# Hymba block in float32 on one core: weight quarters split in step with the products, a last block in two groups of 256 positions, differences on VectorE

## The chip, the cores and the metric

The kernel runs on one core of a Trainium2 chip. The metric is the device time of one execution in microseconds (us). The engines are TensorE (PE, with its weight loads shown apart as PEld), VectorE (DVE), ScalarE (ACT), GpSimd (POOL) and SyncE (SP), which here issues nearly all DMAs. Each engine takes its instructions in the order in which they were put, and waits at one whose data or buffer isn't ready.

## The reference, cut to what matters

```python
def reference(x, norm1_g, w_in, w_gate_up, b_gate, gla_norm_g, conv_w, w_out,
              norm2_g, w_ffn_gate, w_ffn_up, w_ffn_down, norm_f_g):   # x: (1, 2048, 1024) float32
    h = rmsnorm(x, norm1_g)
    p_q, p_k, p_v, p_g, p_a, c_b, c_c, c_h = split(h @ w_in)
    log_a = log_sigmoid(p_a @ w_gate_up + b_gate) / 16
    o = rmsnorm(gla_chunked(p_q * 64 ** -0.5, p_k, p_v, log_a), gla_norm_g) * silu(p_g)
    o_conv = c_b * causal_depthwise_conv(c_c * c_h, conv_w)
    x = x + concat([o, o_conv]) @ w_out
    h2 = rmsnorm(x, norm2_g)
    x = x + (silu(h2 @ w_ffn_gate) * (h2 @ w_ffn_up)) @ w_ffn_down      # hidden width 2816
    return rmsnorm(x, norm_f_g)
```

## The kernel before

Features lie on the 128 partitions and positions along the free axis, in blocks of 512. Two blocks are a half. The stages are the input projection with the two mixers (gated linear attention and the short convolution), the output projection, the FFN's up stage, its down stage and the last norm, and the first four of them run half by half.

**Products.** Float32 operands are split into a high and a low part of the type fp32r, and one product of 128 by 128 weights is three matmuls over 512 columns: high by high, high by low, low by high (L460, L461 and L462 in `product_step`). The big products are made in units. A unit has 2 by 2 blocks of weights and 2 by 2 blocks of operands (two feature blocks by two position blocks) and follows Strassen and Winograd with seven products in place of eight, in the order A11·B11, S1·T1, S2·T2, A12·B21, S3·T3, S4·B22, A22·T4. Each has four steps of three matmuls in the projections and the up stage, and two or three steps in the down stage. A PSUM bank takes each product's sum; ACT copies the first ones out (`copied`, L500), and DVE adds the others to these copies (`plus`, L489). In the down stage all of them are added on DVE.

**Weights.** One DMA of 768 KB or 1 MB (L148, `raw_weights`) brings the four quarters of a unit. `unit_weights` makes the sums of quarters that Strassen and Winograd need on DVE (`mix`, L435) and splits each of the seven results with `weight_quarter`: ACT rounds it to the high part (L193), DVE subtracts to the low one (L194). The pool `wq` holds four such split quarters and the pool `raw` two units' raw weights. A unit's seven splits stand in the program ahead of its products; how far each engine takes them up early is left to the scheduler, which orders each engine's instructions by a simulated timeline. `behind(...)` and `issue_after` add an order of issue, without a wait, on top of it.

**Operands.** The operand sums T1 to T4 are made by `combine` (differences: `subtract`, L359). Those of the second half's projection, and of the second half's FFN (`load_h2`), are stored to DRAM and loaded again, partly to be split again on arrival (L193 with `op<-op`).

**The last block.** The FFN's last unit (`last_unit`) isn't made with seven products: it makes feature blocks 6 and 7 of position blocks 2 and 3 of the four blocks (j = 0 and 1 in the code) as plain products, four columns of 36 matmuls over 512 positions in all: two for j = 0, two for j = 1. Then come, for each j, the add to the residual (L1508), the square (L1511), sums of squares over all features by matmuls of one column (L1454), the factor 1/sqrt by Ln, Exp and a Newton step (`factors`, L1463 to L207), its spreading over the partitions (L1467, transposes L1474, a copy for POOL L1475), eight scalings (L1480) on DVE and POOL and eight stores on SP.

## Time and profile before

| | us |
|---|---|
| median of 3 runs | 2055.72 (2054.32 to 2055.76) |
| the profiled execution, its own time | 2050.15 |
| its span in the trace | 2048.4 |
| PE busy | 2021.6 (99%) |
| DVE busy | 1549.0 (76%) |
| ACT busy | 971.7 (47%) |
| POOL busy | 335.4 (16%) |
| DMA | 422.54 MB, mean 206 GB/s |

A group of instructions is shown as line, engine, operation, output<-input by the program's names, shapes, count | busy us, mean ns of one | idle time of the engine ahead of them, and what ended most of it. A row of waits reads: engine, what waited <- what it waited for: us in all, times, the longest. In a timeline the bracket at a row's end is the idle time ahead of the instruction and what ended it. A matmul's shown length is that of its whole passage, and successive ones overlap; the distance between their starts is what each costs.

### The profile page before, as it was taken

Reading aid. Unit: us, or ns where it says so; the run is one execution under the profiler, and the core shown is the slowest. Engines: PE = TensorE matmul, PEld = TensorE weight load, DVE = VectorE, ACT = ScalarE, POOL = GpSimd, SP = SyncE. Lnnn points to the kernel's source line nnn. Section 1 sums busy time; section 2 is a strip of 40 time slices with the busy share of each in tenths; the row PEclk is TensorE's granted clock in tenths of the full one; section 3 lists DMA queues with packets and bytes.
Section 4 is the critical chain, followed back from the end, with each engine's and each line's share of the span. In section 5 each row is a group of like instructions: output and inputs, shape, how many; then the busy total and the mean of one; then the engine's idle time right before and its main releaser. Section 6 shows DMA issues by size and latency. Waiting matters only on the chain.

```text
span 2048.4 us, 26987 instructions
## 1 busy us (share of the span) xinstructions
PE 2021.6 (99%) x9271; PEld 1662.2 (81%) x9271; DVE 1549.0 (76%) x2533; ACT 971.7 (47%) x1930; POOL 335.4 (16%) x218
## 2 busy tenths in 40 slices
PE   9999999999999999999999999999999999999997
PEld 8788878887888888888788888877888888888886
DVE  7888967558744797778777688877777768778884
ACT  6664556755533344444444452334534443453344
POOL 0000000000002451222222112200311321211213
PEclk9999999999999999999999999999999999999998
DMA  7356886425586873546445576576444434586663
GB/s 262 123 201 215 295 301 188 132 85 160 180 307 233 324 270 134 194 150 216 176 145 193 212 285 250 188 277 273 155 169 170 167 136 170 185 328 221 236 231 114
DMA packets 189738, 422.54 MB, mean 206 GB/s; under 512 B 19904, under 2 KB 65184, under 8 KB 180128
## 3 DMA queue, kind: packets, MB, share of 16 engines
q1 hardware_dynamic: 189600, 420.81, 58.5%
q8 instruction: 73, 1.20, 0.2%
q14 instruction: 65, 0.53, 0.1%
HBM read 276.02 MB, written 144.70 MB: 205 GB/s over the span
## 4 chain that ended last, share of the span: by engine, by line
PE 87%; DVE 4%; DMA 4%; ACT 2%; issue 1%; SPq 1%; POOL 0%; DVEq 0%; ACTq 0%; POOLq 0%
PE mm L460 25%; PE mm L462 25%; PE mm L461 25%; PE mm L1220 2%; PE mm L1221 2%; PE mm L1223 2%; DMA raw<-in_wffn_dram 1%; DVE wq L194 1%; DVE h L894 1%; PE a_ps L976 1%; PE mm L756 1%; PE mm L758 1%; PE mm L757 1%; DMA raw<-in_win_dram 1%; PE o_ps L1144 1%
## 5 line engine op out<-in xcount | busy, mean ns | idle before, releaser
L460 PE MATMUL mm<-op,wq 128*128 128x512 f32 x2467 | 961.5, 392 | 10.9 <-ACT c L500 5.0
L461 PE MATMUL mm<-op,wq 128*128 128x512 f32 x2467 | 959.7, 390 | 0.2 <-DVE op L194 0.2
L462 PE MATMUL mm<-op,wq 128*128 128x512 f32 x2467 | 948.7, 390 | 0.9 <-DVE wq L194 0.6
L193 ACT ACTIVATE wq<-raw 128x512 fp32r<-128x512 f32 (+2 forms) x612 | 355.7, 587 | 582.5 <-PE mm L462 461.3
L194 DVE TENSOR_TENSOR wq<-raw,wq 128x512 fp32r<-128x512 f32 (+2 forms) x612 | 446.8, 736 | 165.1 <-ACT wq L193 163.5
L460 PEld LDWEIGHTS mm<-op,wq 128*128 128x128 f32 x2467 | 463.5, 188 | 115.3 <-ACT c L500 6.8
L462 PEld LDWEIGHTS mm<-op,wq 128*128 128x128 f32 x2467 | 463.5, 188 | 99.6 <-DVE wq L194 2.7
L461 PEld LDWEIGHTS mm<-op,wq 128*128 128x128 f32 x2467 | 463.6, 188 | 96.4 <-DVE op L194 1.7
L1202 POOL TENSOR_TENSOR ssx<-ssx,q 128x512 f32<-128x512 f32 x52 | 75.7, 1473 | 866.4 <-ACT q L1201 866.2
L489 DVE TENSOR_TENSOR c<-mm,c 128x512 f32<-128x512 f32 x196 | 134.6, 687 | 52.3 <-PE mm L462 44.9
L489 DVE TENSOR_TENSOR y<-mm,y 128x512 f32<-128x512 f32 x185 | 126.3, 686 | 47.8 <-PE mm L462 47.5
L435 DVE TENSOR_TENSOR raw<-raw 128x512 f32<-128x512 f32 (+2 forms) x192 | 151.9, 794 | 2.9
L1336 POOL TENSOR_TENSOR t<-c,c 128x512 f32<-128x512 f32 x44 | 74.4, 1690 | 434.8 <-DVE c L1332 406.9
L500 ACT ACTIVATE c<-mm 128x512 f32<-128x512 f32 x198 | 115.6, 587 | 17.5 <-PE mm L462 13.9
L435 DVE TENSOR_TENSOR s<-raw 128x512 f32<-128x512 f32 (+2 forms) x96 | 62.0, 645 | 52.0 <-DMA raw<-in_wffn_dram 36.5
L1220 PE MATMUL mm<-op,wq 128*128 128x512 f32 x256 | 101.2, 396 | 0.0
L1221 PE MATMUL mm<-op,wq 128*128 128x512 f32 x256 | 99.7, 390 | 0.0
L193 ACT ACTIVATE wq<-s 128x512 fp32r<-128x512 f32 (+2 forms) x96 | 56.3, 586 | 90.9 <-PE mm L462 88.2
L1418 POOL TENSOR_TENSOR y<-x,y 128x512 f32<-128x512 f32 x32 | 57.7, 1803 | 230.4 <-DVE y L489 181.3
L1223 PE MATMUL mm<-op,wq 128*128 128x512 f32 x256 | 80.0, 390 | 0.0
L435 DVE TENSOR_TENSOR raw<-s,raw 128x512 f32<-128x512 f32 (+2 forms) x96 | 69.8, 727 | 2.0
L552 ACT ACTIVATE c<-c 128x512 f32<-128x512 f32 x78 | 49.2, 631 | 34.7 <-DVE c L489 32.7
(229 smaller groups left out, 1788.5 us busy)
## 6 DMA issues: line engine op xcount, KB each, us to landing
raw<-in_wffn_dram SPq DMA_DIRECT2D x44, 1024.0 KB, 6.1
sa_B<-so SPq DMA_DIRECT2D x47, 512.0 KB, 4.3
op<-sa_B SPq DMA_DIRECT2D x47, 512.0 KB, 6.9
raw<-in_win_dram SPq DMA_DIRECT2D x22, 1024.0 KB, 5.5
sa_T<-so SPq DMA_DIRECT2D x44, 512.0 KB, 3.8
op<-sa_T SPq DMA_DIRECT2D x44, 512.0 KB, 6.4
raw<-in_wdown_dram SPq DMA_DIRECT2D x24, 768.0 KB, 5.8
sx<-y SPq DMA_DIRECT2D x48, 256.0 KB, 4.4
```

The costliest lines, as they stand in the source:

```text
L193: last_hi[:] = [act.activation(hi, src, AF.Copy)]
L194: last_lo[:] = [dve.tensor_tensor(lo, src, hi.bitcast(F32), ALU.subtract)]
L435: dve.tensor_tensor(*args)
L460: pe.matmul(o[:], wh, xh, start=first and k == 0, stop=False, skip_group_check=True)
L461: pe.matmul(o[:], wh, xl, start=False, stop=False, skip_group_check=True)
L462: return pe.matmul(o[:], wl, xh, start=False, stop=k == n - 1, skip_group_check=True)
L489: last_plus[:] = [dve.tensor_tensor(t[:], o[:], t[:], ALU.add)]
L500: last_out[:] = [act.activation(t[:], o[:], AF.Copy)]
L1202: pool.tensor_tensor(ssq[:], ssq[:], q[:], ALU.add)
L1220: pe.matmul(o[e, j][:], wh, m[:, 0, :], start=k == 0, stop=False)
L1221: pe.matmul(o[e, j][:], wh, m[:, 1, :], start=False, stop=False)
L1223: pe.matmul(o[e, j][:], wl, ops[k][j][:, 0, :], start=False, stop=k == KD - 1)
```

## The change

There are three parts.

1. `subtract` in `combine` puts all differences on DVE. Before, they went to POOL outside a stage in which `with_marks` is set.

2. For most units (nine of the first half's projection, all twelve of the second half's, and all units of the FFN in both halves) the weights no longer come from `unit_weights` but from a generator `weight_flow` that runs through all of them in one line. It makes one quarter's job at a time, and a job needs a credit: there are four at the start, and each product gives one back when its copy or add has been issued (`freed`; for units of 256 columns two quarters share a buffer, and every second product gives one). Each job is issued behind the last copy and the last add (`behind(last_out + last_plus)`), and a quarter's sums go into the same job: the first sum behind A11's split, the next two ahead of S1's split. The raw weights of the next unit are loaded where the jobs of the present unit begin. `load_h2` and `ffn_down` tie their loads to other raw loads accordingly.

3. `last_unit` divides the second of its position blocks into two groups of 256 (p0, p1; the first block is j0). Their columns are made by 72 matmuls over 256 positions in place of 36 over 512. Each engine's order is written out by hand (`then`), all of p1 is scaled on DVE, and its stores alternate between the queues of SP and ACT, as are those of p0 that POOL scales put on ACT's queue.

```diff
         def subtract(y, a, b):
             with behind(last_plus if with_marks else []):
-                (dve if with_marks else pool).tensor_tensor(y, a, b, ALU.subtract)
+                dve.tensor_tensor(y, a, b, ALU.subtract)
...
+    def weight_flow():
+        following = Begun(plan.popleft())
+        while following is not None:
+            u, following = following, None
+            begun_units.append(u)
+            if plan:
+                following = Begun(plan.popleft())
+            raw, w, n = u.raw, u.w, u.raw.shape[-1]
+            a11, a12, a22, a21 = [raw[:, i, :] for i in range(4)]
...
+                jobs = [
+                    ("A11", a11, [(s1, a21, a22, ALU.add)]),
+                    ("S1", s1, [(a21, a11, a21, ALU.subtract), (a11, s1, a11, ALU.subtract)]),
+                    ("S2", a11, ()), ("A12", a12, ()),
+                    ("S3", a21, [(a12, a12, a11, ALU.subtract)]), ("S4", a12, ()),
+                    ("A22", a22, ()),
+                ]
+            for i, (name, part, sums) in enumerate(jobs):
+                yield not (u.narrow and i % 2)
+                with behind(last_out + last_plus):
+                    if name == "S1":
+                        for job in sums:
+                            dve.tensor_tensor(*job)
+                    w[name] = weight_quarter(part)
+                    if name != "S1":
+                        for job in sums:
+                            dve.tensor_tensor(*job)
...
+        def freed(i):
+            if flows and flowing:
+                if not current.narrow or i % 2 or i == len(PRODUCTS) - 1:
+                    credits[0] += 1
+                advance()
...
         oa = mul(0)
         c11 = copied("c11", oa, (0, 0))
+        freed(0)
...
-    def last_unit(src, ops, b12, y, ssq):
-        raw = raw_weights(src)
-        w = [weight_quarter(raw[:, i, :]) for i in (0, 1, 3, 2)]
+    def last_unit(ops, b12, y, ssq):
+        w = [begun_units[0].w[i] for i in (0, 1, 3, 2)]
+        HB = PB // 2
+        parts = {"j0": (0, 0, PB), "p0": (1, 0, HB), "p1": (1, HB, HB)}
...
+        taken("p1", 0, columns_of("p1", 0))
+        add_up("p0", ssq[1])
+        factors("p0", lambda: scale("j0", 1, dve, sp))
+        gained_in("p1", 0)
+        summed("p1", 0, dve)
+        o = columns_of("p1", 1)
+        spread("p0", copied=False)
+        add_up("p1", ssq[1], last=False)
+        taken("p1", 1, o)
+        add_up("p1", q[1, 1], first=False)
+        for d in (3, 7):
+            scale("j0", d, dve, sp)
+        factors("p1", *[partial(scale, "p0", d, dve, sp) for d in (0, 1)])
+        copy_of("p0")
+        gained_in("p1", 1)
+        for d in (2, 5, 6, 7):
+            scale("p0", d, pool, ac)
+        scale("p0", 3, dve, sp)
+        spread("p1", copied=False)
+        scale("p0", 4, dve, sp)
         for d in range(KD):
-            scale(1, d, None if d in (2, 5) else rb1)
+            scale("p1", d, dve, ac if d % 2 else sp)
```

Since a scheduler sets the order, three places show what moves. The first is on ACT in the second half's projection. `ee` are decay factors loaded from DRAM, which ACT turns into exponentials for the attention; `c12` is the third copy of a unit, and `wq` are weight splits. Before:

```order
L1105 ACTIVATE ee_4889<-ee_4889 128x256 [waits DMAHW5_49]
L1106 ACTIVATE ee_4889<-ee_4889 128x256 [waits Activation_49]
L193 ACTIVATE wq_4806<-raw_4784 128x512 [waits DVE_49]
L193 ACTIVATE wq_4809<-raw_4784 128x512 [waits PE_49]
L193 ACTIVATE wq_4998<-raw_4995 128x512 [waits DMAHW7_49,PE_49]
L1023 ACTIVATE el_4741<-g2_4745 128x4 [waits DVE_49]
L1105 ACTIVATE ee_5037<-ee_5037 128x256 [waits DMAHW5_49,DMAHW4_49]
L1106 ACTIVATE ee_5037<-ee_5037 128x256 [waits Activation_49]
L500 ACTIVATE c12_4872<-mm_4812 128x512 [waits DVE_49]
```

Here the copy stands last, behind both pairs of exponentials and four other rows. With the change:

```order
L193 ACTIVATE wq_4856<-raw_4473 128x512 [waits DVE_49]
L1104 ACTIVATE el_4758<-g2_4762 128x4 [waits DVE_49]
L574 ACTIVATE c12_4871<-mm_4804 128x512 [waits DVE_49,PE_49]
L193 ACTIVATE wq_4873<-raw_4473 128x512
L193 ACTIVATE wq_4916<-raw_4671 128x512 [waits DMAHW7_49,PE_49]
L1187 ACTIVATE ee_4894<-ee_4894 128x256 [waits DMAHW5_49,DMAHW1_49]
L1188 ACTIVATE ee_4894<-ee_4894 128x256 [waits Activation_49]
L193 ACTIVATE wq_4935<-s1_4878 128x512 [waits DVE_49,PE_49]
L1187 ACTIVATE ee_5029<-ee_5029 128x256 [waits DMAHW6_49,DMAHW5_49]
L1188 ACTIVATE ee_5029<-ee_5029 128x256 [waits Activation_49]
```

The copy of `c12` stood behind the exponentials of two `ee` tiles, and now stands ahead of both. (The line numbers differ between the two kernels: L500 became L574, L1105 and L1106 became L1187 and L1188.)

The second place is on DVE where the first half's down stage ends and the second half's up stage begins. `y` are the adds of the down stage's products, `s1` and `raw` the sums of quarters, and the wait on DMAHW2_49 is that of the raw weights of the first up unit. Before:

```order
L489 TENSOR_TENSOR y_11037<-mm_12455,y_11037 128x512 [waits PE_49]
L194 TENSOR_TENSOR wq_12544<-raw_12532,wq_12544 128x384 [waits Activation_49]
L435 TENSOR_TENSOR s1_12719<-raw_12717 128x512 [waits DMAHW2_49,DVE_49]
L435 TENSOR_TENSOR raw_12717<-raw_12717 128x512 [waits DVE_49]
L489 TENSOR_TENSOR y_11115<-mm_12560,y_11115 128x512 [waits PE_49]
L194 TENSOR_TENSOR wq_12547<-raw_12532,wq_12547 128x384 [waits Activation_49]
L435 TENSOR_TENSOR raw_12532<-raw_12532 128x384 [waits DVE_49]
```

Here both sums of the new unit stand ahead of an add and of the low part `wq_12547`. With the change (L489 became L557, L435 became L494):

```order
L494 TENSOR_TENSOR raw_12384<-raw_12384 128x384 [waits DVE_49]
L557 TENSOR_TENSOR y_11147<-mm_12567,y_11147 128x512 [waits PE_49,Pool_49]
L194 TENSOR_TENSOR wq_12578<-raw_12384,wq_12578 128x384 [waits Activation_49]
L557 TENSOR_TENSOR y_11145<-mm_12552,y_11145 128x512 [waits PE_49]
L194 TENSOR_TENSOR wq_12591<-raw_12384,wq_12591 128x384 [waits Activation_49]
L557 TENSOR_TENSOR y_11145<-mm_12597,y_11145 128x512 [waits PE_49]
L494 TENSOR_TENSOR s1_12596<-raw_12489 128x512 [waits DMAHW2_49]
L194 TENSOR_TENSOR wq_12608<-raw_12489,wq_12608 128x512 [waits Activation_49]
```

The sum `s1` of the new stage's first unit now stands behind the last low part (`wq_12591`) and three adds of the old stage's last unit.

The third place is SP's queue where the second half's projection begins: loads of stored operands (`op<-si...`), the stores of the mixer's results (`sm`), small attention loads (`gt`), and a unit's raw weights. Before:

```order
L148 DMA op_2864<-siB21_3_456 128x1024 [waits DMAHW5_49,PE_49]
L148 DMA op_2866<-siT3_0_457 128x512 [waits DMAHW6_49,PE_49]
L148 DMA op_2868<-siT3_1_458 128x512 [waits DMAHW7_49,PE_49]
L151 DMA sm0_2_203<-hi_2811 128x512 [waits DMAHW0_49,Activation_49]
L148 DMA op_2870<-siT3_2_459 128x512 [waits DMAHW1_49,PE_49]
L148 DMA op_2872<-siT3_3_460 128x512 [waits DMAHW2_49,PE_49]
L151 DMA sm0_2_203<-c11_2398 128x512 [waits DMAHW3_49,DVE_49]
L148 DMA op_2874<-siB22_0_461 128x512 [waits DMAHW4_49,PE_49]
L148 DMA op_2876<-siB22_1_462 128x512 [waits DMAHW5_49,PE_49]
L148 DMA op_2878<-siB22_2_463 128x512 [waits DMAHW6_49,PE_49]
L148 DMA op_2880<-siB22_3_464 128x512 [waits DMAHW7_49,PE_49]
L148 DMA raw_3044<-in_win_dram 128x2048 [waits DMAHW0_49]
```

Here the raw weights come last. With the change, first the rows from the raw weights on:

```order
L148 DMA raw_2760<-in_win_dram 128x2048 [waits DMAHW5_49,DVE_49]
L148 DMA gt_3081<-sg0_0_153 128x128 [waits DMAHW6_49]
L148 DMA op_2886<-siT3_0_457 128x512 [waits DMAHW7_49,PE_49]
L148 DMA op_2888<-siT3_1_458 128x512 [waits DMAHW0_49,PE_49]
L148 DMA op_2890<-siT3_2_459 128x512 [waits DMAHW1_49,PE_49]
```

The loads of T3 now follow the raw weights. Two rows further on, on the same queue, come the loads of B22 up to the store of `c11`:

```order
L148 DMA op_2894<-siB22_0_461 128x512 [waits DMAHW4_49,PE_49]
L151 DMA sm0_2_203<-hi_2831 128x512 [waits DMAHW5_49,Activation_49]
L148 DMA op_2896<-siB22_1_462 128x512 [waits DMAHW6_49,PE_49]
L148 DMA op_2898<-siB22_2_463 128x512 [waits DMAHW7_49,PE_49]
L148 DMA op_2900<-siB22_3_464 128x512 [waits DMAHW0_49,PE_49]
L151 DMA sm0_2_203<-c11_2390 128x512 [waits DMAHW1_49,DVE_49]
```

The raw weights' load (1 MB) went from behind the loads of B22 to ahead of those of T3, and the store `sm0_2<-c11` from ahead of the four loads of B22 to behind them. Two loads of `gt` were moved up between them.

250 lines of the change are left out of this document (173 added, 77 removed).

## The prediction

> **What bounds the kernel now.** I read the busy times first, then TensorE's waits, then the chain of waits at the end, and last the timeline around each longer wait.
>
> ```profile
> span 2048.4 us, 26987 instructions
> PE 2021.6 (99%) x9271; PEld 1662.2 (81%) x9271; DVE 1549.0 (76%) x2533; ACT 971.7 (47%) x1930; POOL 335.4 (16%) x218
> ```
>
> TensorE is the bound, so the change can win only where TensorE stands still, or where nothing is left for it, at the end. Its waits by cause:
>
> ```profile
> PE mm L460 <- ACT c L500: 5.0, 3, 3.0
> PE mm L460 <- ACT op L193: 2.1, 1, 2.1
> ...
> PE mm L460 <- DVE c L489: 1.5, 3, 0.7
> PE mm L460 <- ACT wq L193: 1.2, 3, 0.5
> ...
> PE mm L460 <- DVE y L489: 0.8, 1, 0.8
> PE mm L462 <- DVE wq L194: 0.6, 1, 0.6
> ```
>
> These add up to 11.2 us. Only 1.8 us of it (the rows of wq) is TensorE waiting for split weights, so a better pace of splitting has little to win directly. What it can do is move other work on ACT and DVE. The splits themselves run early: in the waits of all engines ACT's splits wait for TensorE to free a buffer, 367 times, 1.5 us each.
>
> ```profile
> ACT wq L193 <- PE mm L462: 549.5, 367, 4.1
> DVE s L435 <- DMA raw<-in_wffn_dram: 36.5, 19, 4.1
> ```
>
> The profiled execution took 2050.15 us for a span of 2048.4, and the median shown is 2055.72. I make the sum on the span and add 2055.72 - 2048.4 = 7.3 us for the median.
>
> **Term 1, the end.** The chain of waits from the last product's add on, and the stores:
>
> ```profile
> 2033.75 0.70 DVE y L1508
> 2034.47 0.64 ACT q L1511
> ...
> 2036.86 0.18 DVE rs L205
> ...
> 2037.46 0.44 DVE rep L1467
> ...
> 2037.94 1.13 PE rb_ps L1474 x4
> ...
> 2041.07 2.39 DVE y L1480 x4
> ```
> ```profile
> L151 SPq DMA_DIRECT2D out_dram<-y x16: 332/405/590, 2032.1 to 2044.4; - x16
> DMA to landing us min/median/max: 2.1/2.5/3.4
> ```
>
> From the add at 2033.75 to the last scaling's end at 2043.46 are 9.7 us, and the stores take the 4.9 us to the end: a queue that issues one store in 0.41 us, then a landing of about 2.5. Half-width operations and pitches come from these rows (the first from the down stage's quarters, the second from TensorE's weight loads in the last 40 us):
>
> ```profile
> L435 DVE TENSOR_TENSOR s<-raw 128x256 f32<-128x256 f32 x8 | 3.3, 417 | 1.5 <-DMA raw<-in_wdown_first_dram 1.5
> L462 PEld LDWEIGHTS mm<-op,wq 128*128 128x128 f32 x33 | 6.2, 188 | 1.3
> ```
>
> The four scalings follow each other at 2.39 / 4 = 0.60 us, so one of 256 should follow at 0.33 (0.417 less the same overlap of 0.09). The new order after the last columns of p1: add 0.42; DVE then scales two whole blocks of j0, 1.28, in which the square and the two last column sums hide; mean and eps 0.17; two scalings of p0 while ACT makes Ln and Exp, 0.75; Newton step 0.60 (three rows like the 0.18 one, with gaps); spreading over 256 positions 0.30; two more scalings of p0, 0.78, beside two transposes (1.13 / 2 = 0.56); eight scalings of p1, 2.75. Sum 7.05, against 9.7: a gain of 2.66. Of the 4.9 us to the end, two queues can save at most the backlog of issues, 2044.4 - 2043.46 and one issue, some 1.3 us. Gain between 2.66 and 4.0, taken 3.3.
>
> Against it stand 72 matmuls over 256 positions for 36 over 512. No row has such a matmul. The 512 ones follow at 0.2265 us (472.56, 472.79 below; 0.227 all over the busy stretches). Half of that, 0.113, is the lower bound; a weight load's 0.188 us for every matmul the upper. 36 matmuls now cost 8.15 us; 72 cost 8.15 at the one, 13.5 at the other bound: between 0 and +5.4. I take 0.12 us, +0.5, since the pitch of 0.2265 shows that a load of 0.188 hides wholly under the matmul ahead of it, and PEld's rows are latencies that may overlap each other as PE's do. The Trainium skill, "TensorE: Matmul & The Clock Gate", section on the back-to-back issue gap, gives an isolated gap of N / 2.4 + 2.5 ns; it would be 216 ns at 512 columns, which the trace's 226 nearly bears out, and 109 at 256, so that 72 would cost 7.9 us (an estimate): -0.3 instead of +0.5. Net term 1: **-2.8**, bounds -4.0 and +2.7.
>
> **Term 2, the stall at 476.** It is the longest of the body. TensorE's and ACT's timeline and the chain there:
>
> ```profile
> 472.56 0.39 PE L460 MATMUL mm<-op,wq 128*128 128x512 f32 x1
> 472.79 0.39 PE L461 MATMUL mm<-op,wq 128*128 128x512 f32 x1
> 476.19 0.53 PE L460 MATMUL mm<-op,wq 128*128 128x512 f32 x1 [3.01 <-ACT c L500]
> ```
> ```profile
> 474.79 0.42 ACT L1105 ACTIVATE ee<-ee 128x256 f32<-128x256 f32 x1 [1.02 <-DMA ee<-sd]
> 475.56 0.58 ACT L500 ACTIVATE c<-mm 128x512 f32<-128x512 f32 x1
> ```
> ```profile
> 472.69 2.02 DMA ee<-sd
> ...
> 476.72 0.43 PE mm L461
> ...
> 479.70 0.40 PE mm L462
> ```
>
> The copy of c12 was ready to run at about 473.2, but on ACT an exponential stood ahead of it that waited for a load. After that TensorE goes at 0.43 us a matmul for nine of them. Cost: 476.19 - 472.79 - 0.23 = 3.17, and 9 x (0.43 - 0.23) = 1.8, together 4.9. In the changed order on ACT the copy stands ahead of both pairs of exponentials, behind one split and one small exponential that were ready. What is late next is the `ee` pair, by the two splits now ahead of it (0.59 us each, L193's row on the page has 587 ns); only the attention's scores wait for it, and these run between the products. I take **-4.9**, bounds -4.9 and 0 (the same order with another wait in front).
>
> **Term 3, DVE's sums and ACT's splits ahead of adds and copies.** At three places DVE's first sum of a new unit waits 4 us for raw weights, and adds and low parts queue behind it; at 1422 a copy stands behind a split:
>
> ```profile
> 1380.56 0.69 DVE L435 TENSOR_TENSOR s<-raw 128x512 f32<-128x512 f32 x1 [4.09 <-DMA raw<-in_wffn_dram]
> 1382.63 0.50 PE L460 MATMUL mm<-op,wq 128*128 128x512 f32 x1 [0.79 <-DVE y L489]
> ```
> ```profile
> 1422.56 0.50 PE L460 MATMUL mm<-op,wq 128*128 128x512 f32 x1 [1.69 <-ACT c L500]
> ```
>
> At 1382 TensorE lost 0.8; at 1010 and 1015, in the up stage, 0.6 each (the rows of 0.7 and 0.6 among the waits above). In the changed order the sum stands behind the old unit's last low part, and the raw weights are asked for a unit earlier: -2.0, bounds -2.0 and 0. At 1422 the copy goes one split forward but stays behind a `sg` operation that itself waits for TensorE: -0.5 of 1.7, bounds -1.7 and 0. Together **-2.5**.
>
> **Term 4, the start of the second half's projection.** Here the change loses.
>
> ```profile
> 266.58 5.26 DMA sm<-c
> ```
> ```profile
> 271.87 0.60 ACT L500 ACTIVATE c<-mm 128x512 f32<-128x512 f32 x1 [0.39 <-DMA sm<-c]
> 273.03 0.51 PE L460 MATMUL mm<-op,wq 128*128 128x512 f32 x1 [2.10 <-ACT op L193]
> ```
> ```profile
> 265.00:270.00 5.00, 4.64 (x20) 3.35 (x19) 1.65 (x3) 1.35 (x3) 0.00 (x0) 1.00 1.04 402
> ```
>
> The copy of c12 waits until a tile is free, that is until a store of the mixer's result has landed; behind this copy on ACT stand the splits of T3, and TensorE waits for the first of them (the columns of the last row: PE, PEld, DVE, ACT, POOL, clock, DMA share, GB/s). The DMA engines are full, at 402 GB/s. On SP the change puts the raw weights' 1 MB and the four B22 loads (256 KB each) ahead of that store: 2.1 MB / 0.402 = 5.2 us later. Some slack returns, as the mixer's result may be ready earlier: I take **+4.5**, bounds 0 and +7. The second bound has a second cost in it: after the 3.01 us at 476 the matmuls went at half speed, after the 2.10 us here only the first did. A stall of 6 us would add 1.8 (nine slow ones again). The Trainium skill, the same page, the section on what is actually happening at the clock gate, puts half speed behind an idle window of about 3.4 us; the row at 476 shows it after 3.01 already, so by either this stall would be followed by slow matmuls.
>
> **Term 5, differences on DVE.**
>
> ```profile
> L359 POOL TENSOR_TENSOR t<-h,t 128x512 f32<-128x512 f32 x16 | 25.2, 1573 | 42.5 <-DVE so L194 34.7 <-DVE op L194 6.4 <-DVE h L894 1.4
> L359 DVE TENSOR_TENSOR t<-h,t 128x512 f32<-128x512 f32 x8 | 5.5, 684 | 0.0
> ```
>
> 32 operations like the first leave POOL, and 32 of 0.68, 22 us, come to DVE. 20 of them lie between 690 and 736 us; there TensorE waits for nothing, and the operands made are for the FFN behind it. The stretch around them:
>
> ```profile
> 680.00:760.00 80.00, 80.00 (x354) 66.22 (x353) 71.75 (x80) 31.05 (x54) 41.79 (x26) 1.00 0.83 288
> ```
>
> DVE has 8.3 us free for 20 x 0.684 = 13.7 more: 0 if its backlog drains before the operands are wanted, +5.4 if not. I take **0**, since each difference is also done 0.9 us sooner.
>
> **Sum.** -2.8 - 4.9 - 2.5 + 4.5 + 0 = -5.7: a span of 2042.7, a median of **2050.0**, 0.28% less.
>
> **Rivals.**
> *The boundary costs nothing* (term 4 is 0): the store that frees the tile may come from a result that is ready well before. For it: the result is made by ACT and DVE, which have other orders now. Against: full DMA engines. 2045.5. Chance 0.14.
> *The gains don't come*: the order of the issue changes, but the splits land where they did, since they were held by TensorE's buffers (1.5 us a wait) and still are; new exponentials or loads stand ahead of copies. Then only term 1 is left: 2052.9; with term 4 beside it at +4.5 and half of term 2, 2055. Chance 0.22.
> *Low parts come late in the down stage*, the case on the slower side. Each split is now bound behind the last copy and add of its product, where before it could be taken up sooner. In the down stage DVE has least room (107.1 of 130 us):
>
> ```profile
> 1240.00:1370.00 130.00, 129.86 (x569) 106.05 (x568) 107.08 (x182) 43.39 (x83) 24.38 (x14) 1.00 0.63 230
> ```
>
> A product there has nine matmuls, 2.04 us. Four quarters are held, so a split may be three products, 6.1 us, late before TensorE waits; from there on it decides. One such wait cost 0.6 us (the row of L462 above); one in each of the 24 down units of three steps is 14.4: 2042.7 + 14.4 + 7.3 = 2064.4. Against it: in this stretch TensorE was idle 0.14 us in all. Chance 0.14.
>
> **How the numbers follow.** The forecast has 0.50, its own range is 2045 to 2055, about two thirds of it under 2051.6. A measurement of this kernel tells about 0.2%, 4.1 us, from no change: faster is below 2051.6, slower above 2059.8. Faster: 0.36 of the forecast's, 0.14, and 0.06 of the third case: 0.56. Slower: 0.14, and 0.03 for a boundary stall at its bound together with late differences: 0.17. The same: 0.27. The range, 2041 to 2061, goes below for term 1 at -4.0 with no boundary loss and above for the pitch at 0.188 with the boundary at +7.
>
> **What would show it.** Right: no wait of TensorE at the place of 476 and full clock behind it; a wait of 5 to 8 us at about 273 whose chain goes back to a store `sm<-c`; 256-wide matmuls 0.11 to 0.13 us apart; 10.5 to 12 us from the last add to the end. Wrong: DVE's low parts among TensorE's longest waits, copies still behind exponentials, a 256-wide pitch near 0.19, or a boundary with no longer wait than now.

## The result, and the profile after

| | us |
|---|---|
| before, median of 6 runs | 2054.38 (2050.22 to 2055.76) |
| changed, median of 6 runs | 2065.78 (2059.35 to 2068.62) |
| ratio, with its 95% interval | 1.0055 [1.0045, 1.0066] |
| changed, span of the profiled execution | 2063.6 (before 2048.4) |

The change makes the kernel slower, by 11.3 us as the ratio goes. The prediction said faster, 2050.0, and its range ended at 2061. The profiled spans differ by 15.2 us, since the profiled execution of before (2050.15) lay 4.2 us below its median.

The head of the changed kernel's page:

```profile
span 2063.6 us, 27077 instructions
PE 2027.7 (98%) x9295; PEld 1663.4 (81%) x9295; DVE 1529.3 (74%) x2580; ACT 968.6 (47%) x1936; POOL 281.5 (14%) x189
```

No engine does noticeably more work: DVE's and POOL's busy times fell, TensorE's rose by 6.1 us. What grew is waiting, and matmuls that run slowly behind a wait. TensorE's waits by cause:

```profile
PE mm L523 <- ACT op L193: 10.2, 4, 7.6
PE sc L1200 <- DVE kq L1190: 2.3, 1, 2.3
...
PE mm L523 <- ACT c L574: 2.0, 3, 1.2
PE mm L1302 <- DVE y L1327: 1.7, 2, 1.1
PE mm L523 <- ACT wq L193: 1.5, 2, 1.3
PE mm L525 <- DVE wq L194: 1.4, 3, 0.8
```

(L523 to L525 are now what L460 to L462 were.) Waits for copies `c` shrank from 5.0 to 2.0 us, as forecast; waits for ACT's operand splits `op` grew from 2.1 to 10.2, and those of the attention's scores (`sc`) and the output projection (L1302) are new.

Where the time went is seen when the same DVE add is looked up in both traces:

| add (output) | before, starts at | changed, starts at | changed later by |
|---|---|---|---|
| c22, first half's projection | 119.35 | 119.03 | -0.3 |
| c11, behind the second half's start | 322.58 | 328.71 | +6.1 |
| c11, ahead of the old stall at 476 | 425.68 | 430.74 | +5.1 |
| c22, behind it | 507.37 | 511.76 | +4.4 |
| c22, behind the output projection | 794.17 | 800.65 | +6.5 |
| c12, first half's up stage | 1023.03 | 1028.88 | +5.9 |
| y, first half's down stage, late | 1390.69 | 1399.40 | +8.7 |
| c12, second half's up stage | 1447.41 | 1460.46 | +13.1 |
| c11, the same stage, late | 1730.35 | 1743.50 | +13.2 |
| y, second half's down stage, late | 2007.83 | 2024.91 | +17.1 |
| end of the span | 2048.4 | 2063.6 | +15.2 |

The largest steps are the second half's projection start (+6.4) and the entry of the second half's up stage (+4.3 between 1391 and 1447); the two down stages give 2.9 and 3.9. The tail gives 1.9 back. Each column is one execution, so a small step means little: the kernel of `last_unit_only` (below) has the same instructions as the one before up to the last block, and in its trace the add of 2007.83 starts at 2012.87, 5.0 us later, of which 3.1 come between 1023 and 1391.

**The projection's start.** The chain of waits and two windows there (columns of the windows: PE, PEld, DVE, ACT, POOL, clock, DMA share, GB/s):

```profile
271.72 4.61 DMA sm<-c
...
276.91 0.62 ACT wq L193
277.53 0.53 ACT op L193
278.10 0.80 PE mm L523
278.91 0.79 PE mm L524
279.70 0.43 PE mm L525
```
```profile
272.00:277.00 5.00, 0.00 (x0) 0.00 (x0) 0.69 (x1) 1.70 (x4) 0.00 (x0) 0.81 1.00 362
277.00:282.00 5.00, 3.89 (x9) 2.76 (x10) 4.44 (x8) 5.00 (x11) 0.00 (x0) 0.51 0.97 324
```

The store that frees the copy's tile goes out at 271.72 in place of 266.58, 5.1 us later. It isn't the only one. Two copies on ACT now wait for a store each, the first of them for `sm<-hi`, which goes out at 269.47 (263.78 before); before, only one copy waited, for 0.39 us.

```profile
273.85 0.60 ACT L574 ACTIVATE c<-mm 128x512 f32<-128x512 f32 x1 [8.91 <-DMA sm<-hi]
...
276.41 0.60 ACT L574 ACTIVATE c<-mm 128x512 f32<-128x512 f32 x1 [1.45 <-DMA sm<-c]
```

TensorE stands for 7.6 us. The granted clock is 0.51 in the second window, and most of the matmuls in it start 0.43 us apart instead of 0.2265.

**The entry of the second half's up stage.** TensorE's timeline, and ACT's row on which its second wait rests:

```profile
1408.13 0.47 PE L523 MATMUL mm<-op,wq 128*128 128x512 f32 x1 [1.29 <-ACT wq L193]
1415.63 0.49 PE L523 MATMUL mm<-op,wq 128*128 128x512 f32 x1 [1.81 <-ACT op L193]
...
1434.59 0.50 PE L523 MATMUL mm<-op,wq 128*128 128x512 f32 x1 [1.18 <-ACT c L574]
1438.82 0.50 PE L525 MATMUL mm<-op,wq 128*128 128x512 f32 x1 [0.77 <-DVE wq L194]
```
```profile
1414.95 0.63 ACT L193 ACTIVATE op<-op 128x512 fp32r<-128x512 f32 x1 [2.24 <-DMA op<-shT]
```

Where before had waits of 0.55 and 1.69 us, there are four: for a weight split that was made only just before, for an operand whose load landed late, for a copy and for a low part.

**The lead of the splits.** Among the waits of ACT one row has changed more than the others shown so far:

```profile
ACT wq L193 <- PE mm L525: 172.2, 148, 3.5
ACT wq L193 <- DVE raw L490: 129.4, 60, 5.3
ACT wq L193 <- DVE raw L494: 58.5, 28, 3.6
```

Before, ACT's weight splits waited 549.5 us in 367 waits for TensorE to free a buffer: they were early. Now only 172.2 us are left, and 187.9 us of waiting for DVE's sums (48.6 before) have come instead.

**The end.** DVE's and POOL's timeline in the tail:

```profile
2045.84 0.42 DVE L1638 TENSOR_TENSOR ssx<-ssx,q 128x256 f32<-128x256 f32 x1 [0.61 <-ACT q L1628]
...
2049.30 0.93 DVE L1575 COPY rep<-py 128x256 f32<-128x256 f32 x1
2050.15 1.48 DVE L1638 TENSOR_TENSOR ssx<-ssx,q 128x256 f32<-128x256 f32 x1
2051.56 0.41 DVE L1627 TENSOR_TENSOR y<-mm,y 128x256 f32<-128x256 f32 x1
...
2054.44 0.29 DVE L1575 COPY rep<-py 128x256 f32<-128x256 f32 x1
```
```profile
2046.30 5.06 POOL L1598 TENSOR_TENSOR y<-y,ssx 128x512 f32<-128x512 f32 x4 [3.21 <-ACT ssx L1592]
```

The same copy takes 0.29 us and, while POOL scales, 0.93; the same sum of squares 0.42 and 1.48. The last add (2051.56) thus begins some 1.6 us after its product is done (at 2049.92).

### The profile page after: what moved, and what is told of

Read it like the earlier page. It is cut to its first block, busy times and chain, and to the rows that moved or that the text cites. A ratio compares the mean times of both kernels' runs of the same rounds, so it can differ in the third digit from the quotient of the medians.

```text
span 2063.6 us, 27077 instructions
## 1 busy us (share of the span) xinstructions
PE 2027.7 (98%) x9295; PEld 1663.4 (81%) x9295; DVE 1529.3 (74%) x2580; ACT 968.6 (47%) x1936; POOL 281.5 (14%) x189
## 4 chain that ended last, share of the span: by engine, by line
PE 90%; DMA 4%; DVE 4%; issue 1%; ACT 1%; SPq 0%; DVEq 0%; ACTq 0%
PE mm L523 25%; PE mm L525 25%; PE mm L524 25%; PE mm L1302 3%; PE mm L1305 3%; PE mm L1303 3%; DMA op<-sa_B 1%; DMA op<-shT 1%; DMA op<-sa_T 1%; DVE wq L194 1%; PE a_ps L1057 1%; PE mm L837 1%; PE mm L839 1%; PE mm L838 1%; PE o_ps L1224 1%
## 5 line engine op out<-in xcount | busy, mean ns | idle before, releaser
L523 PE MATMUL mm<-op,wq 128*128 128x512 f32 x2443 | 957.8, 393 | 15.2 <-ACT op L193 10.2
L525 PE MATMUL mm<-op,wq 128*128 128x512 f32 x2443 | 930.2, 390 | 1.5 <-DVE wq L194 1.4
L194 DVE TENSOR_TENSOR wq<-raw,wq 128x512 fp32r<-128x512 f32 (+2 forms) x612 | 434.3, 728 | 211.7 <-ACT wq L193 208.7
L523 PEld LDWEIGHTS mm<-op,wq 128*128 128x128 f32 x2443 | 459.2, 188 | 121.3 <-ACT op L193 12.9
L525 PEld LDWEIGHTS mm<-op,wq 128*128 128x128 f32 x2443 | 459.1, 188 | 101.6 <-DVE wq L194 5.6
L193 ACT ACTIVATE wq<-raw 128x512 fp32r<-128x512 f32 (+2 forms) x612 | 344.8, 584 | 357.8 <-DVE raw L490 129.4
L574 ACT ACTIVATE c<-mm 128x512 f32<-128x512 f32 x198 | 117.8, 595 | 217.1 <-PE mm L525 202.5
L557 DVE TENSOR_TENSOR c<-mm,c 128x512 f32<-128x512 f32 x196 | 134.8, 688 | 113.6 <-PE mm L525 106.7
L557 DVE TENSOR_TENSOR y<-mm,y 128x512 f32<-128x512 f32 x185 | 126.8, 686 | 58.6 <-PE mm L525 58.0
L1418 POOL TENSOR_TENSOR t<-c,c 128x512 f32<-128x512 f32 x44 | 68.2, 1550 | 497.1 <-DVE c L1414 473.5
L1302 PE MATMUL mm<-op,wq 128*128 128x512 f32 x256 | 101.8, 398 | 1.7 <-DVE y L1327 1.7
L194 DVE TENSOR_TENSOR wq<-s,wq 128x512 fp32r<-128x512 f32 (+2 forms) x96 | 68.2, 710 | 0.6 <-ACT wq L193 0.6
L494 DVE TENSOR_TENSOR raw<-raw 128x512 f32<-128x512 f32 (+2 forms) x96 | 64.1, 667 | 1.7
L194 DVE TENSOR_TENSOR op<-op 128x512 fp32r<-128x512 f32 x94 | 62.8, 706 | 3.4 <-ACT op L193 3.1
```

The costliest lines, as they stand in the source:

```text
L193: last_hi[:] = [act.activation(hi, src, AF.Copy)]
L194: last_lo[:] = [dve.tensor_tensor(lo, src, hi.bitcast(F32), ALU.subtract)]
L523: pe.matmul(o[:], wh, xh, start=first and k == 0, stop=False, skip_group_check=True)
L525: return pe.matmul(o[:], wl, xh, start=False, stop=k == n - 1, skip_group_check=True)
L557: last_plus[:] = [dve.tensor_tensor(t[:], o[:], t[:], ALU.add)]
L574: last_out[:] = [act.activation(t[:], o[:], AF.Copy)]
```

## The experiments

All times against runs of the kernel before on the same chip; the last column is (ratio - 1) x 2053. Rows from different chips are compared by their ratios; an interval of 0.001 to either side is 2 us.

| run | us | ratio [95%] | us gained or lost |
|---|---|---|---|
| sub_only | 2051.01 | 0.9989 [0.998, 0.9999] | -2.3 |
| flow_projection_only | 2059.03 | 1.0023 [1.0014, 1.0033] | +4.7 |
| flow_ffn_only | 2059.78 | 1.003 [1.0017, 1.0042] | +6.2 |
| last_unit_only | 2052.62 | 0.9999 [0.999, 1.0008] | -0.2 |
| projection_boundary_order | 2054.45 | 1.0006 [0.9997, 1.0016] | +1.2 |
| projection_flow_unbound | 2051.91 | 0.9994 [0.9985, 1.0003] | -1.2 |
| ffn_flow_unbound | 2056.61 | 1.0018 [1.0008, 1.0027] | +3.7 |
| ffn_operand_splits_late | 2063.06 | 1.0046 [1.0031, 1.0061] | +9.4 |
| change_without_binding | 2049.45 | 0.9983 [0.9974, 0.9992] | -3.5 |
| three_parts_without_ffn_flow | 2044.55 | 0.9961 [0.9949, 0.9974] | -8.0 |
| last_unit_sum_on_tensore | 2049.19 | 0.998 [0.9971, 0.9988] | -4.1 |
| binding_on_scalare_only | 2057.1 | 1.0017 [1.0007, 1.0026] | +3.5 |
| binding_on_vectore_only | 2055.1 | 1.0007 [0.9998, 1.0016] | +1.4 |
| unbound_sum_on_tensore | 2049.56 | 0.9981 [0.9972, 0.999] | -3.9 |
| change_with_boundary_order | 2062.5 | 1.0045 [1.003, 1.006] | +9.2 |
| whole_boundary_both | 2061.58 | 1.0045 [1.0027, 1.0062] | +9.2 |
| unbound_raw_at_fifth_job | 2049.53 | 0.9981 [0.9972, 0.999] | -3.9 |

### The parts one by one

Each of the four parts alone on the kernel before: the differences (the first hunk of the diff), the flow in the projection, the flow in the FFN, and the last block's groups.

```diff
-                (dve if with_marks else pool).tensor_tensor(y, a, b, ALU.subtract)
+                dve.tensor_tensor(y, a, b, ALU.subtract)
```

> The kernel before with the first part alone: all differences on VectorE. Theory (the loss comes from the loads of weights and of operands, and the differences are hidden): within 2 us of before, and no wait of TensorE for VectorE of more than 0.5 us between 520 and 800 us. Rival (VectorE, which has 8.3 us free between 680 and 760, becomes the bound there, or the output projection's adds come late): slower by 2 to 5 us, with the new waits of TensorE for the adds of the output projection (1.7 us in the changed kernel) in this run too.

> The kernel before with the weight flow in the input projection alone; FFN, differences and last unit as before. Theory (raw weights asked for a unit earlier stand ahead of operand loads and of the mixer's stores on a full DMA): a stall of 6 to 8 us where the second half's projection begins (2.1 before), behind it half clock, and in all +3 to +6 us, since the stall at 476 goes, but a wait for the attention's scores of 2 to 3 us comes. Rival (the flow is harmless here, and the boundary's loss comes from the differences moved to VectorE, which reorder everything around it): a stall at the boundary of 2 to 3 us, and a gain of 3 to 5 us in all.

> The kernel before with the weight flow in the FFN alone; projection, differences and last unit as before. Theory: the two waits at 1010 and 1015 go (-1.5 us), each down stage loses 3 to 4 us by TensorE's waits for operands loaded from DRAM, and the entry into the second half's up stage loses 4 to 6 us: +9 to +12 us in all. Rival (the order of the whole FFN depends on where the scheduler stands when it begins, and the loss in the changed kernel is carried over from the projection and the differences): between -3 and +3 us.

> The kernel before with the new last unit alone. Theory (the tail's gain is real, but VectorE's operations of 256 columns take 0.9 to 1.5 us where they run beside GpSimd's scalings, so that the last add waits behind one): -1.5 to -2.5 us, the last add 1.2 to 1.5 us after the last product's end. Rival (the late add came from the flow's other order, not from GpSimd): -2.8 to -4 us, the last add within 0.2 us of the last product's end.

The flows are switched off stage by stage by giving a unit its own source again, as before the change (against the changed kernel, here in the up stage):

```diff
-            us = unit(None, ops)
+            us = unit(wffn[2 * m], ops)
```

The two flows lose 4.7 and 6.2 us (9 to 12 were expected of the FFN's), the differences gain 2.3, and the last block is even by the times, though its trace wins 2.2 us behind the add of 2007.83 (1.5 to 2.5 were expected). TensorE's waits in the output projection come with the projection's flow (1.8 us in its run) and not with the differences: `sub_only` shows no wait of TensorE between 520 and 800 us.

The sum of the parts is +8.4 against +11.3 [9.2, 13.6] for the whole. It counts one gain three times. The waits at 1010 and 1015 us, which the prediction gave to the flow, are gone in `sub_only`, in `flow_projection_only` and in `flow_ffn_only` alike, and each of these traces wins the same 1.8 us there; counted once, the sum would be some +12 (an estimate from these figures). So no one part can be named as what removes these waits.

### The binding taken out

```diff
-                with behind(last_out + last_plus):
+                with behind([]):
```

> The weight flow in the input projection alone, without the order that binds each job behind the last copy and the last add. Theory (what loses is the binding: it holds splits back, with them the release of raw buffers, and so moves loads on the queue): the stall at the second half's start is at most 4 us, and the time within 2 us of before. Rival (what loses is the credits' pace and the raw weights asked a unit ahead): the stall stays at about 8 us and the time at +4 to +6 us over before.

> The weight flow in the FFN alone, without the order that binds each job behind the last copy and the last add. Theory (the binding loses): within 2 us of before, TensorE's waits in the two down stages and the entry into the second half's up stage together within 2 us of those before. Rival (the credits' pace loses): +5 to +7 us over before, as in flow_ffn_only.

> The whole change, but a weight job of the flow is no longer bound behind the last copy and the last add of the step before it; all else (the flow in both stages, the differences on VectorE, the last block's two groups) as in the changed kernel. Theory (the binding is the larger part of the loss, the rest of the flow costs something only in the FFN): the parts measured so far add up to -2.3 (differences) -0.7 (last block) -1.2 (projection flow unbound) +3.7 (FFN flow unbound) = -0.5 us, so a ratio between 0.998 and 1.001 and no stall over 5 us at the second half's projection start. Rival (the loss comes from having the differences on VectorE together with the flow, not from the binding): the ratio stays at 1.004 or more.

Three times the same line is taken out: in the projection it turns +4.7 into -1.2, in the FFN +6.2 into +3.7, and in the whole change +11.3 into -3.5. That is 14.8 us, more than the 5.9 and 2.5 of the parts. In the FFN alone it ends between the theory (within 2 us of before) and the rival (5 to 7). TensorE's first waits at the second half's start, in the projection's flow with the binding and then without, and the waits of ACT's splits in the whole change without it:

```profile
278.33 0.80 PE L528 MATMUL mm<-op,wq 128*128 128x512 f32 x1 [8.13 <-ACT op L195]
```
```profile
273.25 0.50 PE L533 MATMUL mm<-op,wq 128*128 128x512 f32 x1 [0.77 <-ACT wq L198]
275.14 0.50 PE L535 MATMUL mm<-op,wq 128*128 128x512 f32 x1 [1.15 <-DVE wq L199]
```
```profile
ACT wq L198 <- PE mm L535: 523.4, 342, 4.0
...
ACT wq L198 <- DVE raw L504: 21.4, 10, 4.7
ACT wq L198 <- DVE raw L500: 20.6, 7, 4.6
```

The lead is back (523.4 and 342 against 172.2 and 148 above), and the loss is gone. Where it was is seen with the adds of the table above, looked up in the trace without the binding too:

| us gained or lost in the trace | changed | without the binding |
|---|---|---|
| second half's projection start (119 to 323) | +6.4 | -1.9 |
| first half's down stage (1023 to 1391) | +2.9 | +2.4 |
| entry of the second half's up stage (1391 to 1447) | +4.3 | +0.5 |
| second half's down stage (1730 to 2008) | +3.9 | +4.5 |
| from there to the end | -1.9 | -2.1 |

(What stands ahead of such an add can differ between the two by up to five matmuls, 1.1 us.) The binding's price lies at the two starts of a stage. The losses of the down stages stay without it, so they aren't its price (and the first is no larger than the 3.1 us by which two executions of the same instructions differ there).

The loads ahead of the second start are as fast with the binding as without. The add that starts at 1383.08 in the changed kernel starts at 1373.51 without the binding, so the windows are set 10 us apart to show the same work, first of the changed kernel, then without the binding:

```profile
1373.00:1393.00 20.00, 20.00 (x90) 16.57 (x89) 13.87 (x25) 5.08 (x10) 0.00 (x0) 1.00 0.79 255
1393.00:1410.00 17.00, 15.71 (x70) 12.73 (x69) 10.14 (x16) 5.18 (x9) 0.00 (x0) 1.00 1.01 383
1410.00:1420.00 10.00, 7.93 (x31) 5.32 (x30) 5.08 (x9) 5.52 (x10) 0.00 (x0) 1.00 0.98 351
```
```profile
1363.00:1383.00 20.00, 19.08 (x85) 15.47 (x83) 11.87 (x22) 4.74 (x9) 0.00 (x0) 1.00 0.78 258
1383.00:1400.00 17.00, 16.37 (x72) 13.58 (x73) 11.74 (x20) 5.14 (x10) 0.00 (x0) 1.00 1.03 416
1400.00:1410.00 10.00, 9.46 (x42) 7.48 (x41) 8.58 (x15) 6.86 (x14) 0.00 (x0) 1.00 1.06 407
```

In the first 20 us the DMA engines move 255 GB/s with the binding and 258 without it. In the 27 us behind they are full in both and move 1.1 MB less with the binding (383 and 351 GB/s against 416 and 407). Whether this makes the operand's load late there (the wait at 1414.95 above) isn't shown.

### One bound at a time

```diff
-                with behind(last_out + last_plus):
+                with behind(last_out):
```

and `behind(last_plus)` in the second run. `last_out` holds back what is on ACT, `last_plus` what is on DVE.

> The whole change, each weight job bound behind ScalarE's last copy of the step before it, but not behind VectorE's last add. Theory (the high parts are ScalarE's and are what the products, and the stores in SP's queue, wait for, so this bound is the one that loses): ratio 1.003 to 1.006, the stall at the second half's projection start still 4 us or more. Rival (VectorE's bound loses, since the weight sums and low parts stand behind the adds that follow the products): ratio 1.000 or less, stall at the start below 2 us.

> The whole change, each weight job bound behind VectorE's last add of the step before it, but not behind ScalarE's last copy. Theory: ratio 1.001 or less, no stall over 4 us at the second half's projection start. Rival: ratio 1.003 to 1.006 and the stall there.

For ACT's bound neither side came true: the ratio lies between the two, and the wait at the projection's start is 4.8 us, as the theory had it. For DVE's the theory's figures came true (1.0007, and no wait over 0.8 us at that start). But neither bound is free: against -3.5 without a bound, ACT's costs 7.0 us and DVE's 4.9, both together 14.8. At the projection's start ACT's trace loses 5.2 us and DVE's 1.2. ACT's splits again, with the bound on ACT, then on DVE:

```profile
ACT wq L198 <- PE mm L535: 476.9, 300, 4.0
...
ACT wq L198 <- DVE raw L500: 20.0, 10, 4.4
```
```profile
ACT wq L198 <- PE mm L535: 237.4, 192, 8.8
...
ACT wq L198 <- DVE raw L500: 117.2, 54, 4.8
ACT wq L198 <- DVE raw L504: 61.3, 29, 3.6
```

It is the bound on DVE that takes the lead away: the quarters' sums then stand behind the adds, and the splits wait 117.2 and 61.3 us for them. The bound on ACT keeps most of the lead, brings back the wait at the projection's start, and costs no less. So the lead that this row shows isn't the whole price; why ACT's bound brings that wait back isn't worked out.

### The projection's start mended

```diff
-            ops[n] = [(load_undivided if n in WHOLE else load_pair)(p) for p in src[n]]
+            with behind(mix_store if n == "B22" else []):
+                ops[n] = [(load_undivided if n in WHOLE else load_pair)(p) for p in src[n]]
+            if n == "B22":
+                op_mark[:] = [last_load[0]]
...
+                if i == 4 and plan:
+                    with behind(op_mark):
+                        following = Begun(plan.popleft())
```

`mix_store` is the store of `c11`. The next unit's raw weights are also asked for at the fifth of the seven jobs in place of the first, throughout the projection.

> The weight flow in the input projection alone, as in the run flow_projection_only, but at the start of the second half's projection the unit's raw weights are loaded behind the last load of B22, and the loads of B22 stand behind the store of c11. Theory (2.1 MB of loads ahead of that store make it land 5.2 us late): the store goes out some 5 us sooner against the work around it, the stall there falls from 8.3 to about 3 us, the half clock behind it goes, and the time falls by 5 to 7 us against flow_projection_only, to 2052 to 2054. Rival (the copy behind the store was late for another reason, as ACT's splits ahead of it): the stall stays above 6 us, and the time within 2 us of flow_projection_only.

> The whole change with its binding, and only the order at the second half's projection start mended (the next half's raw weights asked for behind its last B22 load, the B22 loads behind the last product's store). Theory (the boundary is one of several places where the binding loses): it saves the 4.6 us that the same mending saved in the projection alone, ratio 1.0025 to 1.004, the stalls around 1410 us still there. Rival (the boundary is the root, what comes later follows from it): ratio 1.001 or less.

> The whole change with its binding; in the projection the next unit's raw weights are asked for at the fifth of a unit's seven jobs and behind the last B22 load, and the B22 loads stand behind the store of the last product's result. Theory (the boundary is one of several places where the binding loses): the stall at the second half's projection start goes from 7.8 to about 4 us, 3.5 to 4.6 us are saved, ratio 1.003 to 1.004, and the waits around 1410 us stay. Rival (the boundary is the root of what comes later): ratio 1.001 or less.

In the projection's flow alone the mending takes 3.5 us of the 4.7, where 5 to 7 were expected; TensorE's wait there falls from 8.1 to 4.2 us, not to 3. In the first of the two runs on the whole change only the store's half was in force: the raw weights were asked for as in the changed kernel, so its expectation names an edit that it doesn't have. With this half alone the wait is 6.5 us in place of 7.6, and the ratio 1.0045. The second has both halves. Its stall at the start is what was expected (the first fence):

```profile
273.99 0.71 PE L533 MATMUL mm<-op,wq 128*128 128x512 f32 x1 [3.93 <-ACT op L198]
```

```profile
286.83 0.50 PE L533 MATMUL mm<-op,wq 128*128 128x512 f32 x1 [2.10 <-ACT wq L198]
```
```profile
287.00:292.00 5.00, 5.00 (x14) 3.44 (x14) 4.28 (x8) 2.91 (x7) 0.00 (x0) 0.66 0.67 184
```

7.6 us became 3.9, and yet the ratio is 1.0045 [1.0027, 1.0062]; the expected 1.003 to 1.004 lies within this interval, but so does no saving at all (1.0055). The waits around 1410 stay, as the theory had it, so the boundary isn't the root of the rest. The second and third fence show where the saving went in the profiled execution (2066.42, the slowest of four): 13 us later TensorE waits 2.1 us for a weight split, where the changed kernel had no wait, and the granted clock falls to 0.66 behind it. An add that starts at 296.47 before is then 7.5 us late, where the changed kernel's is 7.4. Here the mended place handed its wait on to the next.

### What is left in the FFN

```diff
-        unit_splits[:] = last_hi + last_lo
-        with behind(unit_splits):
-            for y, o in unsplit:
-                split(y[:], o[:, 0, :], o[:, 1, :])
-        unsplit.clear()
+        def split_loaded():
+            unit_splits[:] = last_hi + last_lo
+            with behind(unit_splits):
+                for y, o in unsplit:
+                    split(y[:], o[:, 0, :], o[:, 1, :])
+            unsplit.clear()
```

`split_loaded()` is then called behind the unit's last weight split instead of here.

> The weight flow in the FFN alone, binding kept, but the splits of operands that are loaded whole (T3, B22, T4) stand behind the unit's last weight split on ACT, as in the kernel before, not ahead of its last three. Theory that the down stages lose since weight splits queue behind an operand's split that waits for its load: the wait of 0.9 us at 1230 goes, and 1.5 to 3 us of the 6.4 come back. Rival (the operands themselves land late): within 1 us of flow_ffn_only.

> As unbound_sum_on_tensore (whole change without binding, tail's squares on TensorE), but in the FFN the next unit's raw weights are asked for at the fifth of a unit's seven jobs instead of the first. Theory (the raw load stands early on SP's queue, waits there for a buffer that the unit before still reads, and holds up what follows): the FFN flow's price of 4.1 us goes, ratio 0.996 to 0.997, like the run of three parts. Rival (the price comes from the order of sums and splits on VectorE and ScalarE, or the raw weights now come too late): ratio 0.998 or more, and more waits for sums of raw weights.

The first gained nothing (1.0046 against 1.003, intervals that overlap), though the wait at 1230 went (0.78 us in `flow_ffn_only`), so the place of the operand splits isn't what the bound flow loses by. The second, where the FFN asks for the next raw weights at the fifth job instead of the first, came out at 0.9981, the same as without it, as its rival had it. Against the three parts without the FFN's flow (0.9961) that flow costs 4.1 us even unbound, and 3.7 alone. Part of it can be placed. TensorE waits for an add of DVE at the start of each down stage, here in `unbound_sum_on_tensore`:

```profile
1192.27 0.50 PE L533 MATMUL mm<-op,wq 128*128 128x512 f32 x1 [1.26 <-DVE y L571]
...
1833.45 0.50 PE L533 MATMUL mm<-op,wq 128*128 128x512 f32 x1 [1.04 <-DVE y L571]
```

All four traces with the FFN's flow unbound have such a pair, 2.1 to 2.9 us together; the kernel before and the three parts have no wait at these places. Why the add comes late there, and the rest of the 4.1 us, stay open.

### The tail, and the best version

```diff
-        summed("p1", 0, dve)
...
         add_up("p1", ssq[1], last=False)
+        add_up("p1", q[1, 0], first=False, last=False)
```

> Before, with the last block's two groups, and the squares of the second group's next-to-last tile summed by two more column sums of TensorE instead of VectorE's 128x256 add (1.48 us in the changed kernel, while GpSimd scaled tiles beside it). Theory (the tail's last add is late because VectorE's add and copy run long beside GpSimd): the last add begins within 0.6 us of the last matmul, where it was 1.5 us late, and the end comes about 1.0 us earlier than with the last block's change alone, ratio 0.9990 to 0.9997. Rival (whatever VectorE does next at that place is stretched as much, or the chain behind the add sets the end): last add still 1 us or more late, or no gain at the end, ratio within 0.0003 of 0.9999.

> Differences on VectorE, the flow in the input projection alone and unbound, the FFN's weights asked for as before, the last block in two groups; in the tail the squares of the second group's next-to-last tile are summed by two more column sums of TensorE instead of VectorE's add. Theory (the parts are independent): -2.3 -1.2 -0.7, and up to -1.2 more for the tail's add, so 2048.5 to 2050.5 us, ratio 0.9975 to 0.9985. Rival (the parts get in each other's way, because the faster start of one half moves the same loads into a full stretch of the other): 2052 us or more.

> The whole change without the binding, and the tail's squares summed by TensorE: the same as the run of three parts, but with the FFN's weights in the flow. Theory (without the binding the FFN flow costs little once VectorE makes the differences): 1.4 to 3.9 us below the change without binding, so ratio 0.9965 to 0.9977, within 1.5 us of the run of three parts. Rival (the FFN flow costs its +3.7 us of the run alone also here): ratio 0.9978 or more.

DVE's rows in the tail of last_unit_sum_on_tensore, and POOL's scalings beside them:

```profile
2033.28 0.94 DVE L1695 COPY rep<-py 128x256 f32<-128x256 f32 x1
2034.15 0.41 DVE L1747 TENSOR_TENSOR y<-mm,y 128x256 f32<-128x256 f32 x1
```
```profile
2030.28 5.08 POOL L1718 TENSOR_TENSOR y<-y,ssx 128x512 f32<-128x512 f32 x4 [3.22 <-ACT ssx L1712]
```

The copy still takes 0.94 us beside POOL, whose scalings run until 2035.36, but the add that follows it reads one operand from PSUM and takes 0.41. It begins 7.6 us after the first block's column sums are read (at 2026.53) in place of 9.0, so 1.4 us are saved in the tail, where about 1.0 was expected. The times say more than that in one pair of runs (0.998 against 0.9999) and less in the other (0.9981 against 0.9983). In the first pair the instructions are the same up to the last block, and the two traces are 4.0 us apart ahead of it already (the add of 2007.83 starts at 2008.89 and at 2012.87). So the excess lies outside the tail, and no change of the program explains it.

The Trainium skill, "SBUF — State Buffer", section on its two separate sides, says that VectorE and GpSimd hold a shared pair of ports by turns, each for a whole instruction, and that VectorE needs it for operations with two inputs in SBUF and for copies in its two-port mode. The rows agree: the sum with two SBUF inputs begun at 2050.15 ended at 2051.63, 0.27 us after POOL's four scalings (2046.30 + 5.06 = 2051.36), and the add with one input in PSUM wasn't stretched.

The three parts together (differences, unbound flow in the projection, last block with this sum) make 2044.55 us, 8.0 us less than before. Their prices alone add up to -2.3 - 1.2 - 4.1 = -7.6, so nothing shows that they get in each other's way. The gain is larger than the expected 0.9975 to 0.9985, mostly by what the tail's run gave beyond 1.4 us. The three parts beat both kernels, and the whole change without its binding (2049.45) too. With the FFN's flow beside them (`unbound_sum_on_tensore`) the ratio is 0.9981, as that run's rival had it.

## Why the prediction was wrong

**What bounds the kernel.** Right as far as it went: TensorE, which loses time only where it stands. From the row of 549.5 us the prediction took that "a better pace of splitting has little to win directly", and it asked only what other work would move. It didn't ask what is lost when the splits are no longer free to run early. This is the step that failed: the sum has no term for the binding of each job behind the last copy and the last add. It stood only in a rival, at a chance of 0.14, and the order that it makes at the projection's start was priced as a matter of that order alone (term 4). The runs show in its place that the binding costs 14.8 us: the change loses 11.3 with it and gains 3.5 without it. In the traces some 8 of these lie at the second half's projection start and some 4 at the entry of its up stage.

**That rival**, low parts late in the down stage, gave 2064.4 against a measured 2065.78, but by another route than the one that the runs show; that the two numbers lie so near is chance. It put one wait of 0.6 us for a low part into each of 24 down units. TensorE's waits for low parts come to 1.4 us in all, and what the down stages lose (2.9 and 3.9 us) they lose without the binding too (2.4 and 4.5). Its premise, that a split is bound behind the last copy and add, is what the experiments confirm; its place and size aren't.

**Term 1, the end**: predicted -2.8, in the traces -1.9. From the last add's start to the end are 12.0 us, where it had been 14.7, and the 256-wide matmuls mostly follow at 0.116 to 0.121 us (0.12 was taken, of bounds 0.113 and 0.188). What was missed is that two operations of DVE would run long beside POOL; the last add is 1.6 us late by it. Alone the part is worth -0.2 [-2.1, +1.6].

**Term 2, the stall at 476**: predicted -4.9 (its two parts add up to 5.0), the step between 426 and 507 is -0.7. The wait for the copy went, as forecast. What was "late next", the attention's scores, was said to run between the products, and isn't hidden:

```profile
478.84 0.50 PE L523 MATMUL mm<-op,wq 128*128 128x512 f32 x1 [0.56 <-ACT c L574]
486.48 1.07 PE L1200 MATMUL sc<-kq 64*128 64x128 f32 x8 [2.32 <-DVE kq L1190]
```

Behind it come the waits of the output projection (L1302), and by 794 nothing of the gain is left (+1.4 from 426 on).

**Term 3, sums ahead of adds**: predicted -2.5. The wait at 1382 went in the trace. It had no fixed price: in three executions of the same instructions TensorE waits there 0.79 us (before), 1.65 (`last_unit_sum_on_tensore`) and 2.40 (`last_unit_only`). Then 4.3 us are lost between 1391 and 1447, and 0.5 without the binding. The waits at 1010 and 1015 went too, but they go with the differences alone as well.

**Term 4, the projection's start**: predicted +4.5 within 0 and +7, in the traces +6.4. The place and the store were right, and the store was 5.1 us late where 5.2 were worked out. The slack that was to return didn't, and the slow matmuls behind the wait, known to the prediction as its second cost, came with it. But the 2.1 MB aren't confirmed by this. Without the binding the raw weights still go out ahead of the loads of T3 (at 261.38), and the store of `c11` goes out at 267.56, ahead of one load of T3 and those of B22: 1.0 us later than before. TensorE's waits there are then 0.8 and 1.2 us. What was missed is that it is the binding that puts the loads of B22 ahead of the store.

**Term 5, the differences**: predicted 0 by bounds 0 and +5.4, measured -2.3 [-4.1, -0.2]; a gain had been left out of the bounds. Of the 32 operations, 16 and not 20 lie between 690 and 736 us in the trace, 10.9 us in place of 13.7, which brings the term nearer to 0.

**The rivals on the better side.** That the gains don't come was half right: with the waits at 476 and 1382 gone, nothing was won, since other waits came in their place.

## What to carry to other kernels

A row in which an engine waits long and often for buffers is lead: its work is made early. Before such work is tied to the consumer's pace, ask what the first copies and transfers of each stage will wait for; here the tie's price lay at the starts of two stages. Test the order of issue apart from the idea that it came with: the flow of weights did no harm in the projection, and the tie that it was written with lost 14.8 us, far more than all the rest won. Cost a removed wait only together with what is late next, from that thing's own row, and don't take a wait for a load from one execution: the same one was 0.79 us in one and 2.40 in another.

## What the runs showed of the hardware

The half clock: in the 5 us around a wait of 3.9 us at 274 (`whole_boundary_both`) the windows show 0.71, behind the 7.6 us of the changed kernel 0.51 with nine matmuls in 5 us, and behind a wait of 2.1 us at 287 in `whole_boundary_both` still 0.66, while the 2.10 us at 273 before the change slowed only the first matmul. So a wait of 2.1 us may or may not be followed by slow matmuls, and one 13 us behind a longer one was.

A copy of 128x256 took 0.93 to 0.94 us beside POOL's scalings and 0.29 without them, a sum of that shape with both inputs in SBUF 1.48 and 0.42. Adds of that shape with one operand from PSUM took 0.41 and 0.42 us beside the same scalings (2034.15 in `last_unit_sum_on_tensore`, 2047.38 in the changed kernel).
